# The last store of a row-maximum kernel, issued as two halves from two queues

## The chip, the core and the metric

The kernel runs on one core of a Trainium2 chip. The time is device time in microseconds for one execution. Lower is better. A trace of one profiled execution stands beside the times; in it the engines are called PE (TensorE), DVE (VectorE), ACT (ScalarE), POOL (GpSimd) and SP (SyncE). Names with a q at the end, such as SPq, mean the engine's instruction queue, where DMAs are issued and semaphores are waited for.

## The reference

The input is 32 × 512 rows of 1024 numbers in float32, 64 MiB in all. The output is the maximum of each row.

```python
batch, seq, dim = 32, 512, 1024

def reference(x):
    return np.max(x, axis=-1).astype(np.float32)
```

## The kernel before

The 16384 rows are spread over 128 partitions, 128 rows to each. A first block gives each partition 112 consecutive rows, a second block 16. The second block's last two rows are loaded in two pieces of columns each (`PIECES`, 532 and 492 columns, 592 and 432 columns), so that the last maxima are short.

All loads are issued by SP (lines 238 and 243), in the order in which the rows are wanted, into a ring of 47 rows a partition. A load into a place of the ring that is still being read waits for the maxima that read it; `PLAN`, an order written out by hand, fixes the order of all steps. VectorE takes most maxima straight from the ring (`maximum`, line 78). A share of some rows goes another way: TensorE transposes it (line 160), ScalarE copies it from PSUM (line 166), GpSimd takes the maximum over the partitions (line 168), and TensorE turns the result back (line 178), whereupon VectorE joins it to its own part. The last step of the plan, `m99`, takes the maximum over a small tile `joint` for five columns of the result at once.

The results stand in `res`, the first 128 columns of the same tile as the ring, so that the trace calls them `ring`: column i of partition p holds one row's maximum. `views` holds, for each of the two blocks, the place in the output and the columns of `res`. The first block is stored by ScalarE's queue once the first maximum of the pieces is done (line 265; 128 partitions of 112 numbers). The second block is stored from the same queue behind the last maximum (line 267; 128 partitions of 16 numbers, 64 bytes each, 8 KB in all). In the output these 8 KB are contiguous. A DMA issued from SP goes to the queue q1 of the page, one from ScalarE to q10.

At the program's end (line 292 in the trace) SP waits for the semaphores of all DMAs. There are eight of these, and the DMAs take them in turn, so that one semaphore serves several DMAs. Then all engines meet in a closing barrier. The waits stand in SP's queue in pairs; the last two pairs hold, in this order, the semaphore of the first store together with the one that the next DMA in turn would use, and the semaphore of the last store together with VectorE's.

Of the kernel before, what the change touches and what calls it, by code (L numbers as in the profile page):

```python
# [40 lines left out]
def kernel(  # L41
# [5 lines left out]
    nc = tc.nc  # L47
    P = 128
# [28 lines left out]
    def maximum(out, in_):  # L77
# [8 lines left out]
        out=colno, data0=ident, data1=ident, initial=-1.0, op0=ALU.add, op1=ALU.mult))  # L86
    in_turn("DVE", nc.vector.transpose(out=rowno, in_=colno[:, :32]))  # L87
    for q in range(1, P // 32):
        part = rowno[q * 32:(q + 1) * 32, 0:1]
        in_turn("DVE", nc.vector.tensor_scalar(  # L90
            out=part, in0=part, scalar1=float(q * 32), scalar2=None, op0=ALU.add))
    identity = in_turn("DVE", nc.vector.tensor_scalar(  # L92
        out=ident, in0=colno, scalar1=rowno[:, 0:1], scalar2=None, op0=ALU.is_equal))

    loads = []
    views = []
    last = len(PIECES)
    first = at = 0
    for sizes in BLOCKS:
        S = sum(sizes) + last * (sizes is BLOCKS[-1])  # L100
        xb = xf[first * P:(first + S) * P, :].rearrange("(p i) d -> p i d", p=P)
        dst = bass.AP(tensor=of.tensor, offset=of.offset + first * P, ap=[[S, P], [1, S]])
# [161 lines left out]
    for dst, src in views[:-1]:  # L264
        store = nc.scalar.dma_start(out=dst, in_=src)
        tc.add_manual_dep(store.ins, behind.ins.name, SYNC, reason="behind the loads")
    nc.scalar.dma_start(out=views[-1][0], in_=views[-1][1])

# [1 line left out]
_INS = ['x']  # L270
# [26 lines left out]
```

## Time and profile before

| | |
|---|---|
| median of 3 runs | 163.84 us (163.82 to 163.93) |
| profiled execution: span, from the first to the last instruction | 162.1 us |
| its own time beside the span | not given on the page; the median lies 1.74 us above the span |
| VectorE busy | 135.3 us, 83% of the span |
| DMA, queue q1 (loads from SP) | 67.11 MB, 96.8% of 16 engines' span |
| DMA, queue q10 (stores from ScalarE) | 0.07 MB, 0.2% |
| last store (line 267) | issued at 159.86 us, issue 338 ns, 1.4 us from issue to landing |

In the profile, times of single instructions are counted from the span's start. The issue of a DMA is what the issuing engine's queue spends on it; its landing is the last count on its semaphore. The sixteen DMA engines are shared by both queues, and "DMA share" is their mean busy share.

### The profile page before, as it was taken

What the parts mean: (1) busy time and instruction counts of PE and PEld (TensorE: products, weight loads), DVE (VectorE), ACT (ScalarE), POOL (GpSimd) and SP (SyncE); (2) the same over time, 40 slices, a digit from 0 to 9 for tenths busy, and PEclk for the clock granted to TensorE, in tenths of its full rate; (3) what the DMA queues carried; (4) which work ended last, traced back from release to release, by engine and by line L of the source; (5) the groups of instructions that cost most, each with busy time, mean ns of one, the idle gap of its engine ahead of it and who ended that gap; (6) DMA issues with size and microseconds to landing.
All of it is one profiled execution on the core that took longest, in us unless ns stands there. A gap on an engine that the chain in (4) does not pass through costs nothing.

```text
span 162.1 us, 295 instructions
## 1 busy us (share of the span) xinstructions
PE 13.6 (8%) x76; PEld 11.7 (7%) x76; DVE 135.3 (83%) x33; ACT 6.3 (4%) x7; POOL 15.9 (10%) x10
## 2 busy tenths in 40 slices
PE   0000000000000000000000000000000000772942
PEld 0000000000000000000000000000000000762731
DVE  3500019998399999999999999996999999999994
ACT  3000000000000000000000000000000000241120
POOL 0000000000000000000000000000000000099791
PEclk9999999999999999999999999999999999996555
DMA  5995999599879999898999799799999989999991
GB/s 178 566 485 258 470 501 517 259 517 517 354 340 439 453 404 534 356 523 367 478 411 475 334 485 475 334 485 388 477 429 388 466 382 446 415 421 416 411 388 34
DMA packets 3456, 67.18 MB, mean 414 GB/s; under 512 B 640, under 2 KB 896, under 8 KB 1536
## 3 DMA queue, kind: packets, MB, share of 16 engines
q1 hardware_dynamic: 3168, 67.11, 96.8%
q10 hardware_dynamic: 288, 0.07, 0.2%
HBM read 67.11 MB, written 0.07 MB: 414 GB/s over the span
## 4 chain that ended last, share of the span: by engine, by line
DMA 50%; DVE 47%; SPq 1%; issue 0%; DVEq 0%
DMA ring<-in_x_dram 50%; DVE ring L78 45%; DVE joint L78 2%; SPq L238 1%; DVEq L292 0%
## 5 line engine op out<-in xcount | busy, mean ns | idle before, releaser
L78 DVE TENSOR_REDUCE ring<-ring 128x1 f32<-128x1024 f32 (+13 forms) x20 | 129.9, 6547 | 23.5 <-DMA ring<-in_x_dram 23.5
L168 POOL PARTITION_ALL_REDUCE top<-sb x6 | 15.7, 2658 | 142.6 <-ACT sb L166 142.5
L160 PE MATMUL ps<-ident,ring 128*128 128x128 f32 x38 | 9.0, 423 | 140.0 <-DMA ring<-in_x_dram 140.0
L160 PEld LDWEIGHTS ps<-ident,ring 128*128 128x128 f32 x38 | 7.6, 225 | 140.1 <-issue 140.1
L166 ACT COPY sb<-ps 128x1024 f32<-128x1024 f32 (+2 forms) x6 | 5.0, 834 | 150.5 <-PE ps L160 143.5
L78 DVE TENSOR_REDUCE joint<-ring 128x2 f32<-128x1280 f32 (+1 forms) x3 | 3.9, 1314 | 0.0
L178 PE MATMUL got<-ident,top 1*128 1x1 f32 x24 | 2.7, 228 | 3.8 <-POOL top L168 3.6
L178 PEld LDWEIGHTS got<-ident,top 1*128 1x128 f32 x24 | 2.4, 188 | 4.6 <-POOL top L168 4.6
L178 PE MATMUL joint<-ident,top 1*128 1x1 f32 x14 | 2.0, 244 | 1.9 <-POOL top L168 1.9
L178 PEld LDWEIGHTS joint<-ident,top 1*128 1x128 f32 x14 | 1.7, 210 | 2.7 <-POOL top L168 2.7
L166 ACT ACT_TABLE_LOAD x1 | 1.3, 1283 | 0.7 <-PEq L281 0.7
L83 DVE MEMSET ident<- 128x128 f32 x1 | 0.2, 165 | 0.8 <-PEq L281 0.8
L90 DVE TENSOR_SCALAR rowno<-rowno 32x1 f32<-32x1 f32 x3 | 0.4, 146 | 0.1
L85 DVE TENSOR_TENSOR_SCAN colno<-ident 128x128 f32<-128x128 f32 x1 | 0.4, 425 | 0.0
L92 DVE TENSOR_SCALAR ident<-colno,rowno 128x128 f32<-128x128 f32 x1 | 0.3, 288 | 0.0
L87 DVE STREAM_TRANSPOSE rowno<-colno 128x32 f32<-128x32 f32 x1 | 0.2, 211 | 0.0
L78 DVE TENSOR_REDUCE ring<-got 128x3 f32<-128x24 f32 x1 | 0.2, 172 | 0.0
L78 DVE TENSOR_REDUCE ring<-joint 128x5 f32<-128x20 f32 x1 | 0.2, 170 | 0.0
L281 POOL MEMSET const-float32-0.0<- 128x1 f32 x1 | 0.1, 98 | 0.2 <-issue 0.2
L281 POOL MEMSET const-bfloat16-1.0<- 128x1 bf16 x1 | 0.1, 102 | 0.0
L281 POOL MEMSET const-uint8-127<- 128x1 uint8 x1 | 0.1, 101 | 0.0
L281 POOL MEMSET const-float32-1.0<- 128x1 f32 x1 | 0.1, 98 | 0.0
(1 smaller groups left out, 0.1 us busy)
## 6 DMA issues: line engine op xcount, KB each, us to landing
ring<-in_x_dram SPq DMA_DIRECT2D x2, 5632.0 KB, 29.9
ring<-in_x_dram SPq DMA_DIRECT2D x2, 5120.0 KB, 36.8
ring<-in_x_dram SPq DMA_DIRECT2D x2, 4096.0 KB, 32.5
ring<-in_x_dram SPq DMA_DIRECT2D x1, 7680.0 KB, 22.6
ring<-in_x_dram SPq DMA_DIRECT2D x1, 7168.0 KB, 58.0
ring<-in_x_dram SPq DMA_DIRECT2D x3, 1536.0 KB, 35.7
ring<-in_x_dram SPq DMA_DIRECT2D x1, 3584.0 KB, 29.2
ring<-in_x_dram SPq DMA_DIRECT2D x2, 1024.0 KB, 17.8
```

What stands on the lines that cost most here:

```text
L78: return in_turn("DVE", nc.vector.reduce_max(out=out, in_=in_, axis=X))
L83: in_turn("DVE", nc.vector.memset(ident, 1.0))
L85: in_turn("DVE", nc.vector.tensor_tensor_scan(out=colno, data0=ident, data1=ident, initial=-1.0, op0=ALU.add, op1=ALU.mult))
L87: in_turn("DVE", nc.vector.transpose(out=rowno, in_=colno[:, :32]))
L90: in_turn("DVE", nc.vector.tensor_scalar(out=part, in0=part, scalar1=float(q * 32), scalar2=None, op0=ALU.add))
L92: identity = in_turn("DVE", nc.vector.tensor_scalar(out=ident, in0=colno, scalar1=rowno[:, 0:1], scalar2=None, op0=ALU.is_equal))
L160: in_turn("PE", nc.tensor.transpose(out=ps[:, w:w + P], in_=rows(j)[:, lead[j] + r + i, c * P:(c + 1) * P], identity=ident,))
L166: in_turn("ACT", nc.scalar.copy(out=sb[:, :W], in_=ps[:, :W]))
L168: in_turn("POOL", nc.gpsimd.partition_all_reduce(top[:, :W], sb[:, :W], P, bass_isa.ReduceOp.max))
L178: in_turn("PE", nc.tensor.transpose(out=share(j)[:, r + i, c:c + 1], in_=tops[k][0:1, w:w + P], identity=ident[0:1, 0:1],))
L238: load = nc.sync.dma_start(out=rows(issued), in_=src)
L281: nc = _bacc.Bacc("TRN2", target_bir_lowering=False, num_devices=1)
```

## The change

The last store is issued as two DMAs in place of one. Partitions 0 to 63 go from ScalarE's queue, partitions 64 to 127 from SP's queue, each 64 partitions of 16 numbers, 4 KB. Both read the columns that the last maximum completes, so both wait for it. SP's half stands in SP's queue behind the last load and ahead of SP's waits at the program's end; it uses the semaphore that was next in turn, one that also served earlier loads. The first store (line 265) stays as it was.

```diff
     for dst, src in views[:-1]:
         store = nc.scalar.dma_start(out=dst, in_=src)
         tc.add_manual_dep(store.ins, behind.ins.name, SYNC, reason="behind the loads")
-    nc.scalar.dma_start(out=views[-1][0], in_=views[-1][1])
+    dst, src = views[-1]
+    half = P // 2
+    for q, engine in enumerate((nc.scalar, nc.sync)):
+        part = bass.AP(tensor=dst.tensor, offset=dst.offset + q * half * dst.ap[0][0],
+                       ap=[[dst.ap[0][0], half], list(dst.ap[1])])
+        engine.dma_start(out=part, in_=src[q * half:(q + 1) * half])
```

## The prediction

> **What bounds the kernel now.** I read the chain of waits first, to see what the end hangs on. Its columns are start and length in microseconds, and what held the chain. Of its 30 pieces these are the first of the long ones and the last ones:
>
> ```profile
> 1.62 41.49 DMA ring<-in_x_dram
> 43.13 66.55 DVE ring L78 x5
> 111.01 38.94 DMA ring<-in_x_dram
> ...
> 158.57 0.49 DVE ring L78
> 159.05 0.09 issue
> 159.14 0.59 DVE ring L78
> 159.74 0.09 DVEq L292
> ```
>
> For nearly the whole span the chain is load traffic or VectorE's maxima over the loaded rows (line 78). The page gives 50% of the chain to DMA and 47% to VectorE, so the change touches none of what makes the kernel long. The chain as printed stops at 159.83 us of 162.10 us. The 2.27 us behind it are the last store and the program's end, and it is only there that the change can act. The last computing instruction and the store stand in the timeline of the end; "idle before" is empty because nothing is shown as waiting between them:
>
> ```profile
> 159.66 0.17 DVE L78 TENSOR_REDUCE ring<-joint 128x5 f32<-128x20 f32 x1
> 159.86 0.34 ACTq L267 DMA_DIRECT2D out_dram<-ring  x1
> ```
>
> The answer on line 267 gives the store's issue (338 ns) and its time to landing. The table of stretches around it then shows when its bytes move; the last two columns are the busy share of the 16 DMA engines and GB/s:
>
> ```profile
> L267 ACTq DMA_DIRECT2D out_dram<-ring x1: 338/338/338, 159.9 to 159.9; - x1
> DMA to landing us min/median/max: 1.4/1.4/1.4
> ```
>
> ```profile
> 159.86:160.20 0.34, 0.00 (x0) 0.00 (x0) 0.00 (x0) 0.00 (x0) 0.00 (x0) 0.50 0.00 0
> 160.20:160.69 0.49, 0.00 (x0) 0.00 (x0) 0.00 (x0) 0.00 (x0) 0.00 (x0) 0.50 0.00 0
> 160.69:160.91 0.22, 0.00 (x0) 0.00 (x0) 0.00 (x0) 0.00 (x0) 0.00 (x0) 0.50 0.42 38
> 160.91:161.29 0.38, 0.00 (x0) 0.00 (x0) 0.00 (x0) 0.00 (x0) 0.00 (x0) 0.50 0.00 0
> 161.29:162.10 0.81, 0.00 (x0) 0.00 (x0) 0.00 (x0) 0.00 (x0) 0.00 (x0) 0.50 0.00 0
> ```
>
> So the end has five legs, with every engine's compute idle: issue 0.34, silence 0.49 while the queue turns the instruction into packets, 0.22 in which the packets move, 0.38 until the last completion count is seen, and 0.81 of closing barrier. The sum is 2.24 us, from 159.86 to 162.10. Of these the bytes take 0.22 us, and even there the DMA engines are busy for 42% only. Inside these legs the trace's packet and semaphore records are finer: 128 packets of 64 bytes start from 160.694 to 160.890 us at 10.5 ns each; 16 completion packets (one for each DMA engine, about 9 ns each) run from 160.749 to 160.906; the 16 counts reach the store's semaphore one by one from 161.098 to 161.273, about 11 ns apart. SyncE sees the full count at 161.290 and then begins the closing barrier.
>
> Who waits for the store is SyncE (SP) alone, as its own list of waits from 157 us on says (total, times, longest):
>
> ```profile
> SPq L292 <- DMA out_dram<-ring: 2.2, 2, 1.6
> ```
>
> The 162.10 us are one profiled execution; the page gives no device time for it besides its span. The runs have a median of 163.84 us, so 1.74 us lie outside the span, and I carry them over unchanged: what the span gains or loses is added to 163.84. A measurement of this kernel can tell about 0.2%, 0.33 us, from no change; the three runs lie within 0.11 us.
>
> **The change, part by part.** Nothing ahead of 159.83 us moves: the instruction order of TensorE, VectorE, GpSimd and ScalarE is the same in both programs up to the last store, and SP's loads stand as before. The last load is issued at 149.97 us and the new store stands behind it on SP, so it is moved past no load and holds none up.
>
> *The issue on ScalarE.* It stays, for 64 rows in place of 128. The trace has no store or load of 64 rows. What it has: an SP issue right behind a wait takes 327 or 328 ns, whether the rows hold 1728 bytes or 45056 bytes, so bytes do not set it. Whether rows do is not shown. The bounds are 338 ns unchanged (0) and half of it (−0.17 us). I take 0, by the nearest row: the same form of instruction with very different sizes and one price.
>
> *The issue on SP, new.* Both issues wait for the same VectorE count. Line 78 ended at 159.825 and ScalarE started at 159.858, 33 ns later; SP's answer to the same semaphore is 28 ns elsewhere (a maximum ended at 39.936, the load behind it issued at 39.964). So the two start together. The added instruction that waits for the reused load semaphore costs nothing: that load landed near 155.2 us. The issue is 0.33 us, beside ScalarE's of 0.34 us, if the two can be worked on at once: 0. If not, the second comes later by one issue (0.33 us) or by SP's start-to-start spacing of issues without a wait between them. That spacing is in the chain's pieces around 110 us:
>
> ```profile
> 109.69 0.33 SPq L238
> 110.02 0.05 issue
> 110.07 0.42 SPq L238
> 110.50 0.05 issue
> 110.55 0.42 SPq L238
> ```
>
> From 110.07 to 110.55 it is 0.48 us. The bounds are 0 and +0.48. No row of the trace has SP and ScalarE issuing within 1 us of each other, so this is the open price. I take 0, since two instruction streams are the nearest thing to what the trace shows running side by side, but keep +0.48 for the range.
>
> *The silence of 0.49 us.* It follows the issue of 128 rows here, and one of 0.50 us follows the 56 KB store of line 265 (issue ends 158.39, first packet 158.89). Seven times the bytes cost nothing. For 64 rows it could be half, −0.25 us, or the same. I take the same.
>
> *The packets.* The data are still 128 packets of 64 bytes, over the same 16 engines. New are 16 more completion packets of 9 ns, one an engine: +0.01 us. If each half's 0.22 us window came after the other at full length it would be +0.22; if they overlap, 0. The window is the spread of the engines' starts more than it is work (8 packets of 10.5 ns are 0.08 us on an engine), so I take +0.01.
>
> Here a rule of the Trainium skill speaks against the change. "DMA: Bandwidth & Descriptors", section Rules for kernel authors, says of two transfers to disjoint partition halves "Don't bother — they serialize", because both halves use all 16 engines, and that issuing from two engines saves the sequencers' issue time alone. The trace agrees as far as it goes: 0.22 us of 2.24 is all that serializing packets can be about. By the rule the sum has no gain in the packets, which is what it holds without it.
>
> *The landing.* There are 32 counts now, on two semaphores. At the 11 ns spacing shown, one behind the other, the last is 16 × 11 ns = 0.17 us later; side by side, 0. I take half, +0.08 us, since the first store's counts too come in an even 10 ns step (159.430 to 159.596), which looks like a line that both would stand in.
>
> *The waits behind it on SP.* This is the instruction whose queue matters. In the program before, SP has issued its last load at 149.97 us and works off its closing waits while the last maxima run; at 159.61 it passes the last but one, and only one is left for the store. After the change, four of these closing waits stand behind the new store. They are already satisfied and cost about 0.06 us each (161.290 to the next instruction at 161.355): 0.24 us from 160.19 to 160.43, hidden below the 1.1 us until the landing at 161.27. Without that cover they would cost 0.24. One is not hidden: SP waits first for the pair that now holds its own store, then for the pair that holds ScalarE's. If SP's half lands last, the second wait comes 0.065 us later than its count; if ScalarE's half lands 0.065 us later, nothing. I take +0.06.
>
> The sum: 0 (issue) + 0 (silence) + 0.01 (packets) + 0.08 (counts) + 0.06 (one more wait) = +0.15 us, so 163.84 + 0.15 = 163.99 us, +0.09%. With the half-cost issue the case reaches down to 163.84 − 0.17 = 163.67, and with all counts in one line up to 163.84 + 0.01 + 0.17 + 0.06 = 164.08.
>
> **The rivals.** *Slower: the two issues go one behind the other.* One mechanism: what turns an instruction into packets serves one queue at a time, so the second half's packets start one issue later. Price +0.33 to +0.48, plus the wait of 0.06 (and 0.01): 164.24 to 164.39, in the middle 164.32. It decides as soon as the second half's first packet is over 0.26 us behind the first's, since 0.26 + 0.07 is the 0.33 that can be measured. For it: of SP's back-to-back issues those at 110.07 and 110.55 take 0.42 and not 0.33 us, as if something behind the queue were still busy; a second instruction on another queue might meet the same thing. Against it: nothing in the trace shows the two queues meeting.
>
> *Faster: rows are the price.* Issue and silence both go by rows, 0.34 + 0.49 = 0.83 us halves, −0.42, and with the +0.06 of the wait the time is 163.84 − 0.36 = 163.48. For it: the first packets of an issue start engine after engine, as if made in turn. Against it: 0.49 and 0.50 us of silence for 64- and 448-byte rows, and 327 ns whatever the bytes; both look like fixed prices.
>
> *The change does not do what it says*, because SP comes to its store late. The last load before it was issued ten microseconds earlier, and the waits on SP are satisfied, so I see no reason; it would look like the slower rival.
>
> **How the numbers follow.** The halves go side by side: 0.58. One behind the other, or partly so by more than the bound: 0.33. Rows are the price: 0.08. That leaves 0.01 for what I do not see. Of the first case I put nothing outside ±0.33 us. So faster 0.09, same 0.57, slower 0.34. The likeliest time is 163.99 us, with its own range 163.67 to 164.08. The range over the cases goes from 163.60, which leaves the faster rival out (0.08), to 164.40, which takes in the upper price of the slower one and leaves a delay above a full issue spacing out (0.07 or so).
>
> **What would show it.** Right: two issues that both start near 159.86 and last about 0.33 us; no change in the maxima before them; first packets near 160.69 on both queues; the last count at 161.28 to 161.45; a closing barrier of 0.81. The step on the issue is wrong if either issue is well under 0.3 us or above 0.4. The step on the silence is wrong if the packets of one queue start more than 0.1 us before or after 160.69. The slower rival is right if the second half's packets start 0.3 us or more behind the first's. I am wrong altogether if the 1.74 us outside the span move, or if the time before 159.83 does.

## The result and the profile after

| | before | after |
|---|---|---|
| median of 6 runs | 163.86 us (163.82 to 163.99) | 164.42 us (164.30 to 164.44) |
| span of the profiled execution | 162.1 us | 162.6 us (its time 164.38 us) |

The ratio is 1.003 (95% interval 1.002 to 1.004): the change makes the kernel slower by 0.56 us, 0.3%. The prediction had 163.99 us as likeliest, and a rival of 164.24 to 164.39 us. Of its three cases, no change beyond 0.33 us (0.57), faster (0.09) and slower (0.34), the slower one came.

The chain of waits of the changed kernel has the old holders in the old order up to the last maximum, with starts and lengths that differ by 0.07 us at most:

```profile
1.62 41.43 DMA ring<-in_x_dram
43.07 66.56 DVE ring L78 x5
110.96 38.92 DMA ring<-in_x_dram
...
158.50 0.49 DVE ring L78
158.99 0.09 issue
159.08 0.60 DVE ring L78
159.68 0.09 DVEq L297
```

It even ends 0.06 us earlier (159.77 for 159.83), so the loss is all behind it. The timeline of the end has the two new issues:

```profile
159.59 0.17 DVE L78 TENSOR_REDUCE ring<-joint 128x5 f32<-128x20 f32 x1
159.79 0.53 SPq L272 DMA_DIRECT2D out_dram<-ring  x1
159.80 0.54 ACTq L272 DMA_DIRECT2D out_dram<-ring  x1
```

They start together, as the prediction had it, but each takes 0.53 or 0.54 us where the whole store took 0.34. The answers on line 272, first for ScalarE's queue and then for SP's, give the issues in ns and the landings:

```profile
L272 ACTq DMA_DIRECT2D out_dram<-ring x1: 542/542/542, 159.8 to 159.8; - x1
DMA to landing us min/median/max: 2.0/2.0/2.0
```

```profile
L272 SPq DMA_DIRECT2D out_dram<-ring x1: 525/525/525, 159.8 to 159.8; - x1
DMA to landing us min/median/max: 1.7/1.7/1.7
```

ScalarE's half lands last, 2.0 us behind its issue, where the whole store needed 1.4. The stretches of the end (start and end, length, engines, clock, DMA share, GB/s) show where:

```profile
159.79:160.34 0.55, 0.00 (x0) 0.00 (x0) 0.00 (x0) 0.00 (x0) 0.00 (x0) 0.50 0.00 0
160.34:160.95 0.61, 0.00 (x0) 0.00 (x0) 0.00 (x0) 0.00 (x0) 0.00 (x0) 0.50 0.00 0
160.95:161.15 0.20, 0.00 (x0) 0.00 (x0) 0.00 (x0) 0.00 (x0) 0.00 (x0) 0.50 0.22 21
161.15:161.23 0.08, 0.00 (x0) 0.00 (x0) 0.00 (x0) 0.00 (x0) 0.00 (x0) 0.50 0.00 0
161.23:161.42 0.19, 0.00 (x0) 0.00 (x0) 0.00 (x0) 0.00 (x0) 0.00 (x0) 0.50 0.24 22
161.42:161.78 0.36, 0.00 (x0) 0.00 (x0) 0.00 (x0) 0.00 (x0) 0.00 (x0) 0.50 0.00 0
161.78:162.59 0.81, 0.00 (x0) 0.00 (x0) 0.00 (x0) 0.00 (x0) 0.00 (x0) 0.50 0.00 0
```

There are two bursts of packets with a gap between them. By the trace's records the SP queue's first packet comes at 160.960, ScalarE's at 161.230, 0.27 us later, and the first burst is over (161.145) before the second begins. Each burst lasts 0.18 us, hardly less than the 0.21 of the whole store. The legs of ScalarE's half against the whole store are: issue 0.542 for 0.338 (+0.204), silence from the issue's end to its first packet 0.892 for 0.498 (+0.394), data packets 0.180 for 0.207 (−0.027), from the last of these until SP sees the last count 0.368 for 0.389 (−0.021). The sum is +0.55 us. The closing barrier is 0.81 as before. Less the 0.06 of the earlier start this is the span's +0.49.

The waits of SP's own queue, from 157 us on, show that its closing waits cost nothing: those that are satisfied stand below the wait for the store (1.0).

```profile
SPq L272 <- DVE ring L78: 4.8, 1, 4.8
SPq L297 <- DMA out_dram<-ring: 1.2, 2, 1.0
```

So two things need a cause: why a half takes longer than a whole to issue and to start, and why the second half starts 0.27 us behind the first.

### The profile page after: what moved, and what is told of

Same layout as the page of the kernel before. It is cut to its first block, busy times and chain, and to the rows that moved or that the text cites. A ratio compares the mean times of both kernels' runs of the same rounds, so it can differ in the third digit from the quotient of the medians.

```text
span 162.6 us, 297 instructions
## 1 busy us (share of the span) xinstructions
PE 13.4 (8%) x76; PEld 11.6 (7%) x76; DVE 135.3 (83%) x33; ACT 6.3 (4%) x7; POOL 15.9 (10%) x10
## 4 chain that ended last, share of the span: by engine, by line
DMA 49%; DVE 47%; SPq 1%; issue 0%; DVEq 0%
DMA ring<-in_x_dram 49%; DVE ring L78 44%; DVE joint L78 2%; SPq L238 1%; DVEq L297 0%
```

## The experiments

Experiments are edits of the kernel before unless said otherwise; `part(a, b)` is the last store's rows of partitions a to b−1. Differences of time are against the kernel before on the same chip. Landings are from the start of the issue to the last count, by the trace's records. The times are medians and the ratios are not taken from them, so a difference and its ratio can disagree by some 0.05 us. In the cuts of code the removed line is the same throughout, and so is left out after the first; the definition of `part` and the lines that set an option back are left out too.

**Half of the store alone.**

```diff
-    nc.scalar.dma_start(out=views[-1][0], in_=views[-1][1])
+    nc.scalar.dma_start(**part(0, 64))
```

> Only ScalarE's half is stored; the other 64 partitions of the second block are left out. In the changed kernel both issues took 0.53 to 0.54 us in place of 0.34, the first packets came 0.64 (SP) and 0.89 us (ScalarE) behind the end of the issue in place of 0.50, and the last landing 1.97 us behind the issue in place of 1.41. Theory (the two DMAs meet on their way from issue to packets, and each is a fixed charge whatever its rows): alone, the half is as the whole was, issue 0.33 to 0.34, silence 0.5, packets 0.17 to 0.21, landing 1.35 to 1.42, time 163.80 to 163.88. Rival (a DMA of 64 rows is dear by itself): issue 0.53, silence 0.64 or more, landing 1.7 or more, time 164.15 or more. Second rival (rows are the price, and the meeting hides it): issue near 0.17, silence near 0.25, time near 163.5.

Measured: 164.12 us for 163.84 (ratio 1.0017, 1.0008 to 1.0026), with half of the bytes and nothing to meet; the kernel leaves the other half of the second block unwritten. The answer on the store's line:

```profile
L273 ACTq DMA_DIRECT2D out_dram<-ring x1: 512/512/512, 159.8 to 159.8; - x1
DMA to landing us min/median/max: 1.7/1.7/1.7
```

The issue is 0.51, the silence 0.66, the landing 1.70. My theory, that all of it was the meeting, fell: a store of 64 rows is dearer by itself than one of 128, by 0.28 us.

**Both halves from ScalarE's queue.**

```diff
+    nc.scalar.dma_start(**part(0, 64))
+    nc.scalar.dma_start(**part(64, 128))
```

> Both halves from ScalarE's queue, one behind the other. Theory (each DMA is a fixed charge, and two from different queues take turns): first issue 0.34, second 0.42 with a start 0.40 to 0.48 behind it; second half's packets 0.4 to 0.5 us behind the first's; time 163.86 + 0.4 to 0.5 = 164.26 to 164.36, slightly below or at the changed kernel's 164.42. Rival (64 rows are dear by themselves): both issues 0.53 or more, time over 164.8. Rival (halves are cheap and only the two queues' meeting costs): second packets within 0.2 us of the first's, time below 164.1.

Measured: 164.77 us, +0.93 (ratio 1.0056, 1.0044 to 1.0069). The issues are 0.51 and 0.61 us, start to start 0.55, and the second lands 1.79 us behind its issue. The issues are the rival's, dear halves, and the time is just under the 164.8 that it asked for. SP's wait for the second half comes first in its pair order and passes at 162.07; the next wait comes at 162.11. From the last count to the barrier's first instruction 0.12 us pass for 0.08 in the kernel before, so the extra wait that the prediction feared is real where the half on the reused semaphore lands last, and costs 0.04.

**The whole store from SP.**

```diff
+    nc.sync.dma_start(**part(0, 128))
```

> The whole last store from SP's queue, nothing from ScalarE's. Theory (meeting): issue 0.33, silence 0.50, landing 1.4, no second DMA, time 163.82 to 163.90. Rival (SP's queue is slow for stores, or its closing waits, moved behind the store, cost what they take): closing waits 0.24 us later or a longer silence, time 164.1 or more.

Measured: 163.81 us for 163.84 (ratio 0.9998, 0.9989 to 1.0007).

```profile
L273 SPq DMA_DIRECT2D out_dram<-ring x1: 348/348/348, 159.8 to 159.8; - x1
DMA to landing us min/median/max: 1.4/1.4/1.4
```

SP's queue is as good as ScalarE's for a store, and SP's closing waits behind it, from 160.20 to 160.41 us in its records, lie below the landing at 161.22. Neither the queue nor the moved waits is the cause.

**The whole store beside a load of 64 rows.**

```diff
+    spare = once.tile([P, 16], F32)
+    nc.scalar.dma_start(**part(0, 128))
+    load = nc.sync.dma_start(out=spare[64:128, :], in_=xf[64:128, 0:16])
+    tc.add_manual_dep(load.ins, latest["DVE"].ins.name, SYNC, reason="beside the store")
```

> The whole last store from ScalarE's queue as before, and beside it SP issues an unrelated load of 64 partitions of 16 numbers into a spare tile, released by the same last maximum; the output is complete. Theory (any two issues that meet cost, whatever they move): ScalarE's issue 0.5 to 0.55 in place of 0.34, the later one's first packet 1.3 to 1.45 us behind the issue, last landing near 1.9, time 164.3 to 164.5. Rival (two stores into the same 8 KB of output, or a split in halves, are what costs): ScalarE's issue 0.34 and its landing 1.4; time 163.86, or up to 0.06 more for one wait.

Measured: 164.45 us, +0.61 (ratio 1.0034, 1.0021 to 1.0046). The time is what I expected and the reason is not. ScalarE's store first, SP's load second:

```profile
L274 ACTq DMA_DIRECT2D out_dram<-ring x1: 343/343/343, 159.9 to 159.9; - x1
DMA to landing us min/median/max: 1.4/1.4/1.4
```

```profile
L275 SPq DMA_DIRECT2D spare<-in_x_dram x1: 531/531/531, 159.9 to 159.9; - x1
DMA to landing us min/median/max: 1.9/1.9/1.9
```

The store of 128 rows is not touched by an issue 4 ns before its own. It is the DMA of 64 rows that is late, a load here, on the other queue. So dearness goes with 64 rows, in a load as in a store, on SP's queue as on ScalarE's. The load's silence is 0.77 for the 0.66 of the half alone; whether the 0.11 more comes from the neighbour or from being a load, this run does not separate.

**What is special about 64 rows.** The program as built answers it. Each of its DMAs of 128 rows carries a mark, `ant_dge_precooked`; the two halves carry none. By its name the mark says that the DMA's description was prepared ahead; what it does inside no run shows, and the traces show its price alone. I built stores of other sizes: 16, 32, 48, 63, 65, 80, 96, 112, 127 rows are marked; exactly 64 is not, on whichever partitions it starts. The mark can also be kept off (`nc.dge_precook = False`), which makes the test: a chain of stores behind the last one, each behind the landing of the one before.

```diff
+    store = nc.scalar.dma_start(**part(0, 128))
+    for lo, hi, ready in [(0, 128, True), (0, 64, True), (64, 128, True), (0, 48, True), (48, 128, True),
+                          (0, 32, True), (0, 16, True), (0, 96, True), (0, 112, True), (0, 127, True),
+                          (0, 1, True), (0, 128, False), (0, 48, False)]:
+        nc.dge_precook = ready
+        again = nc.scalar.dma_start(**part(lo, hi))
+        tc.add_manual_dep(again.ins, store.ins.name, SYNC, reason="one by one")
+        store = again
```

> Behind the last store, ScalarE issues 13 more stores of parts of the same 8 KB, each behind the landing of the one before (same values again), so the kernel is some 25 us longer; what is asked is the issue and the landing of each. In the built program a DMA of any other number of rows carries a mark that it was prepared ahead; those of exactly 64 rows, on whichever partitions, carry none, and the last two stores of this chain (128 and 48 rows) are built without it on purpose. Theory (the missing mark is the price): issue 0.33 to 0.35 and landing 1.3 to 1.43 for 128, 48, 80, 32, 16, 96, 112 rows; issue near 0.51 and landing near 1.7 for the two of 64 and for the two last. Rival (fewer rows to a DMA engine are dearer): price rises steadily from 128 to 16, the 128 without mark is as cheap as with it. Rival (fewer rows are cheaper but for the 64): landing falls with the rows, 16 rows at 1.2 or below.

Measured, from the trace's records of issues, packets and semaphore counts of one execution, in us; each row is one store (the whole kernel took 184.39):

| rows | marked | issue | silence | packets | landing |
|---|---|---|---|---|---|
| 128 | yes | 0.339 | 0.504 | 0.20 | 1.41 |
| 112 | yes | 0.323 | 0.502 | 0.19 | 1.38 |
| 80 | yes | 0.323 | 0.505 | 0.18 | 1.40 |
| 48 | yes | 0.341 | 0.505 | 0.16 | 1.36 |
| 16 | yes | 0.321 | 0.500 | 0.15 | 1.31 |
| 64 (0 to 63) | no | 0.548 | 0.656 | 0.18 | 1.73 |
| 64 (64 to 127) | no | 0.473 | 0.663 | 0.18 | 1.65 |
| 128 | no, kept off | 0.502 | 0.658 | 0.21 | 1.74 |
| 48 | no, kept off | 0.563 | 0.663 | 0.16 | 1.77 |

At these sizes the mark decides: without it the issue is 0.47 to 0.56 us for 0.32 to 0.34, and the silence 0.66 for 0.50. Rows decide almost nothing: from 128 to 16 of them the landing falls by 0.10 us, 0.08 of it in the packets and the counts. The chain's two odd sizes fall outside this. A store of 127 rows, though marked, took 0.48 us of issue, had one completion packet where those of the table have 16, spread its packets over 0.90 us and landed after 2.6 us; a store of one row took 0.24 and landed after 1.04.

**The whole store without the mark.**

```diff
+    nc.dge_precook = False
+    nc.scalar.dma_start(**part(0, 128))
```

> The kernel before with one edit: the last store, whole and from ScalarE, is built without the mark that it was prepared ahead. Theory (the mark is the price of the 64 rows): issue 0.51 to 0.53, first packet 0.62 to 0.68 us behind the issue's end, landing 1.70 to 1.75; 163.84 + 0.28 = 164.12, within 0.06. Rival (64 rows are dear for their number): issue 0.34, landing 1.41, 163.84.

Measured: 164.10 us for 163.69 on this chip, +0.41 (ratio 1.0027, 1.0018 to 1.0036).

```profile
L274 ACTq DMA_DIRECT2D out_dram<-ring x1: 537/537/537, 159.8 to 159.8; - x1
DMA to landing us min/median/max: 1.8/1.8/1.8
```

With no split at all, losing the mark costs 0.35 us of landing (1.77 for 1.41). The size is above my 0.28: the landing gives 0.35, and the 0.28 is just below the interval of the time (+0.29 to +0.59). The sign and the legs (issue 0.54 for 0.34, silence 0.65 for 0.50) show the cause.

**Another cut, with marks on both parts.** 80 and 48 rows on the two queues.

```diff
+    nc.scalar.dma_start(**part(0, 80))
+    nc.sync.dma_start(**part(80, 128))
```

> The change with another cut: partitions 0 to 79 from ScalarE's queue, 80 to 127 from SP's. Both DMAs carry the mark. Theory (the changed kernel's loss is 0.28 us for the missing mark and 0.27 us for the meeting of two DMAs, and the meeting is shorter for prepared ones): both issues 0.33 to 0.36, first packets of the first near 0.84 us behind its issue, those of the second 0.08 to 0.20 behind that; time 163.92 to 164.04. Rival (the meeting costs 0.27 whatever is prepared): 164.10 to 164.15. Rival (prepared DMAs do not meet at all): 163.80 to 163.90.

Measured: 163.84 us for 163.69, +0.15 (ratio 1.0013, 1.0004 to 1.0022). Issues of 0.36 and 0.38 us and one burst of packets; the stretches from the issue on:

```profile
159.86:160.25 0.39, 0.00 (x0) 0.00 (x0) 0.00 (x0) 0.00 (x0) 0.00 (x0) 0.50 0.00 0
160.25:160.71 0.46, 0.00 (x0) 0.00 (x0) 0.00 (x0) 0.00 (x0) 0.00 (x0) 0.50 0.00 0
160.71:160.94 0.23, 0.00 (x0) 0.00 (x0) 0.00 (x0) 0.00 (x0) 0.00 (x0) 0.50 0.43 36
160.94:161.43 0.49, 0.00 (x0) 0.00 (x0) 0.00 (x0) 0.00 (x0) 0.00 (x0) 0.50 0.00 0
```

First packets come at 160.721 and 160.749, only 0.03 us apart, so marked DMAs hardly meet before the packets. What is longer is the leg behind them, 0.49 us for 0.38: the records have SP's 16 counts from 161.084 to 161.244 and ScalarE's 16 from 161.271 to 161.410, one line behind the other, though the packets overlapped. Both ends of my expectation for the first packets (0.08 to 0.20 apart) were too high. The time is as expected as a difference (+0.08 to +0.20), but for another reason: before the packets the rival was right, by which marked DMAs do not meet, and the counts, which neither had, made up most of the time.

**The same cut on one queue.**

```diff
+    nc.scalar.dma_start(**part(0, 80))
+    nc.scalar.dma_start(**part(80, 128))
```

> The same cut, 80 and 48 partitions, both from ScalarE's queue and both marked. With unmarked halves the second issue took 0.61 us behind a first of 0.51, and the kernel 164.77. Theory: first issue 0.34, second 0.42 to 0.45 behind it, last landing 0.46 to 0.50 us later than the whole store's, time 164.27 to 164.37; two queues (0.08 to 0.20 later) are then cheaper than one queue, and both dearer than one store. Rival (the queue is free as soon as the issue ends, and 48 rows are quick): time below 164.2.

Measured: 164.24 us, +0.55 (ratio 1.0031, 1.0019 to 1.0042). The issues are 0.33 and 0.44, start to start 0.37; the second lands 1.46 us behind its issue. That is a little above the +0.43 to +0.53 that I expected; in the trace the last landing is 0.41 later than the whole store's, and the extra wait of 0.04 is there too. Two queues do spare the second issue (+0.15 for +0.55), and one store is still better than either.

**The 80/48 cut without marks**, and on the same chip the changed kernel and the marked cut again.

```diff
+    nc.dge_precook = False
+    nc.scalar.dma_start(**part(0, 80))
+    nc.sync.dma_start(**part(80, 128))
```

> The split 80/48 on two queues once more, with the mark taken from both DMAs, and nothing else changed; the two parts together are the whole store. Theory (what the changed kernel lost is the missing mark, once by itself and once in the meeting, and the number 64 has no other part in it): issues 0.51 to 0.55, first packets near 1.17 and 1.43 us behind the issue, last landing near 1.95; time over the kernel before as the changed kernel, +0.5 to +0.62 us. Rival (64 rows are dear in a second way): +0.28 to +0.45.

> The changed kernel itself, on the same chip as the split 80/48 without marks, to compare the two: both theories +0.5 to +0.62 us over the kernel before, by its own result.

> The split 80/48 with marks, on the same chip as the changed kernel. Theory: +0.13 to +0.2 us over the kernel before, some 0.4 below the changed kernel; last landing near 1.54 us behind the issue, the second DMA's completion counts standing behind the first's.

Measured, against 163.90 us on this chip: unmarked cut 164.44 (ratio 1.0036, 1.0022 to 1.0049), changed kernel 164.40 (1.0034, 1.0022 to 1.0047), marked cut 164.04 (1.0009, 1.0000 to 1.0018). The issues and landings of the unmarked cut:

```profile
L275 SPq DMA_DIRECT2D out_dram<-ring x1: 594/594/594, 159.8 to 159.8; - x1
L274 ACTq DMA_DIRECT2D out_dram<-ring x1: 577/577/577, 159.8 to 159.8; - x1
...
DMA to landing us min/median/max: 1.6/1.8/2.0
```

(The 1.6 is the first store's.) First packets come at 161.030 and 161.297, 0.27 us apart, as in the changed kernel, where the marked cut on this chip has 0.04. So the mark explains both parts of the loss: an unmarked cut at another place costs as much as the halves, within 0.1 us, which leaves nothing for the number 64 itself. A marked DMA of 64 rows was not run. No version tried beats the kernel before; the whole store from SP equals it.

## Why the prediction was wrong in its likeliest case

*The start, the cover and the barrier held.* Nothing moved ahead of the last maximum, both issues started within 5 ns of each other, SP's satisfied waits lay below the landing (three, from 160.37 to 160.52; the fourth that the prediction counted holds SP's own half), the barrier stayed 0.81, and the outside stayed too: 164.38 − 162.59 = 1.79 us, as in the other runs (1.77 to 1.79). The prediction's 1.74 sets the span of one execution against a median. The reused load semaphore was full at 155.0, not near 155.2, which changes nothing.

*The issue was the step that failed*, taken at 0 and measured +0.20 us, outside its bounds of −0.17 and 0. The step's own sign, an issue above 0.4 us, was met by both. I used the nearest rows, all issues of 128 rows, and concluded from their one price at any size in bytes that the form did not matter. All those rows carried the mark and the new DMAs do not. A bound above zero was missing for ScalarE's issue; I had reasons only for a gain. The mark stood in the built program and I had looked at the order of its instructions alone.

*The silence failed in the same way*: taken as unchanged, measured +0.39 for the half that ends last. By the half alone 0.16 of this is the missing mark (0.66 for 0.50), and 0.23 the turn behind the other half.

*The slower rival was right in sign, and right in size by luck*: the sum asked for 0.26 us between the first packets and 0.27 were measured, but the prediction's list of signs asked for 0.3 or more, which was missed. Its price was one issue, 0.33 to 0.48, and the measured turn is 0.27. A turn of 0.27 alone would have made about half of the loss; the other 0.28 is the missing mark, which the rival did not contain. The median of 164.42 lies 0.02 above the top of the range; as a difference from the kernel before it is at that top (+0.56), which stood for the longest issue spacing and not for these two parts. "Something behind the queue still busy" would fit: unmarked DMAs keep 0.27 us between first packets, marked ones 0.03 to 0.04. Which unit makes the second wait no run here shows.

*The faster rival fell*: rows are not the price, since 16 rows and 112 have the same issue (0.32) and the same silence (0.50).

*The count line exists, but not where the term was added.* In the changed kernel the halves are so far apart that their counts do not meet, so the term is 0 instead of +0.08. Where they overlap, in the marked cut, the leg behind the packets grows by 0.10. The one more wait, taken at +0.06, cost 0, since ScalarE's half landed 0.26 us after SP's.

The +0.15 us of the likeliest case is what the change costs with marked parts: +0.15 and +0.14 were measured. The terms agree less well than the sum. In the trace of the marked cut the counts are +0.10 for +0.08, the issue +0.04 for 0, the packets −0.02 for +0.01, and the one more wait 0 for +0.06, since ScalarE's part landed last again. So the likeliest case has the right size for two marked parts, in part by luck, and what it lacked is the form of the new DMAs.

The rule "Don't bother" in the Trainium skill's "DMA: Bandwidth & Descriptors", section Rules for kernel authors, gave the right advice. The page lays it to packets on the same engines. Here the packet bursts stayed at 0.18 us each, and the loss came before the first packet: +0.20 of issue and +0.39 of silence.

## What to carry to other kernels

The last store of 8 KB is nearly all fixed cost: 0.34 us of issue, 0.50 until the first packet, 0.2 of packets, 0.38 until it is seen. Cutting it divides none of the first two and adds counts, so issue it once, from either queue. Before a DMA is given a new shape, look in the built program whether it still has the form that the trace's prices are for: the same 8 KB landed 0.33 to 0.35 us later without the mark, and 64 rows was the one size built between 16 and 128 that lost it.

## What the runs showed that I had not expected

- A DMA of 64 rows is built without the mark; alone it costs 0.47 to 0.55 us of issue and 0.66 us until the first packet, one of 48 or 80 rows 0.32 to 0.34 and 0.50.
- For marked stores of 16 to 128 rows, in multiples of 16, the price before the packets does not depend on rows: 0.32 us of issue and 0.50 of silence for 16 rows as for 112.
- Two marked DMAs from two queues start their packets 0.03 us apart, two unmarked ones 0.27. The marked ones' completion counts, on two semaphores, come one line behind the other, 9 to 12 ns apart on average, though the packets overlap.
